# Channel mixers: inner tiles 6 to 19 all by seven block products, one weight pair's low half by an adding transfer, the residual parked in DRAM

## The chip, the cores and the metric

The kernel runs on one core of a Trainium2 chip. The metric is device microseconds (us) of one execution. TensorE (PE) multiplies, with its weight loads shown apart as PEld; VectorE (DVE) and ScalarE (ACT) do elementwise work; GpSimd (POOL) and SyncE (SP) here mostly start transfers (DMAs), which all run on the core's 16 DMA engines. Each engine works through its own instruction queue strictly in order. The order in a queue is set when the program is built and does not change at run time.

## What is computed

Two layers on a sequence of 512 positions and 1024 channels. Each has a mixer (layer 0: a recurrent one, layer 1: chunked attention) and then a channel mixer, which is where the change is:

```
def conv_glu(h, w_in, conv_w, conv_b, w_out):
    gate, val = jnp.split(h @ w_in, 2, axis=-1)
    gp = jnp.pad(gate, ((0, 0), (CONV_W - 1, 0), (0, 0)))
    conv = conv_b + sum(conv_w[j] * gp[:, j:j + seq] for j in range(CONV_W))
    return (jax.nn.gelu(conv, approximate=False) * val) @ w_out
...
        x = x + jnp.concatenate([mix, mo], axis=-1) @ w_out[layer]
        x = x + conv_glu(rms_norm(x, ln2[layer]), ffn_in[layer], ffn_conv[layer],
                         ffn_conv_b[layer], ffn_out[layer])
```

The inner width is 2816, that is 22 inner tiles of 128 columns, each with a gate block and a value block of `h @ w_in`. Everything is float32.

## The kernel before

Channels lie on the 128 partitions, positions along the free dimension. A float32 product is made of three matmuls in a faster format (`fp32r`): every operand is split into a high half (a cast, ACT) and a low half (operand minus high half, DVE), and high x high, high x low and low x high are added up in PSUM. `split_w` does this for weights, into buffers `whi` and `wlo` of 1024 columns; three of each rotate. `load_w` loads a weight block into `wraw` (two rotate) and splits it.

`ffn(l, ...)` is the channel mixer of layer `l`. Its loop over the inner tiles `j` has two bodies:

- `plain(j)`: gate and value each as one dense product over all 1024 channels, 24 matmuls of 512 columns each, 48 together. Two weight blocks are loaded and split.
- `seven(j)`: gate and value as a 2x2 block product by a Strassen-like scheme with seven block products (`prod`), 12 matmuls of 256 columns each, 84 together. The four weight blocks G1, V1, G2, V2 (512 columns each) are loaded into a buffer `raw` with room for seven blocks (two such buffers rotate); DVE makes the sums S1 and S3 (line 431, one instruction over two blocks), S2 (line 432) and S4 (line 435); S4 is written over V1. Then the operands are split: three pairs of blocks (1024 columns each) and S4 (512 columns). The four results pass through PSUM banks f1 to f4, and DVE adds them up (lines 443 to 454). The products run in the order G1, S2, S3, S1, V2, G2, S4; below they are P1 to P7.

Tiles 0 to 5 are plain (on the not yet normalised input), as meanwhile `normed` prepares the block sums of the input; of tiles 6 to 19, eleven go by `seven` and tiles 9, 13 and 17 are plain; 20 and 21 are plain. Then the 22 hidden tiles are split (`halves`), and eight output tiles follow, each with three weight loads and 66 matmuls; its result is added to the residual `xT` (line 496), 16 KB on each partition, which lies in SBUF all the time.

A buffer that rotates is loaded again only when its last reader is done. For `raw` the last reader is the split of S4, and V1, the first block to be loaded, lies in the same place. So the load for a tile waits on SP for the DVE half of the S4 split two `seven` tiles earlier. The loads run on SP's queue, in order. A scheduler that works while the program is built, with its own estimates of durations, decides how the instructions of neighbouring tiles are interleaved in each engine's queue.

An adding transfer is already in use elsewhere (`split_w` with `src`, in the projections of layer 0): ACT writes the operand with its sign turned, rounded to `fp32r` like the high half, into `wlo`, and a transfer started by POOL adds the operand, read again from DRAM, to it. This takes the subtraction from DVE.

Of the kernel before, what the change touches and what calls it, by code (L numbers as in the profile page):

```python
# [10 lines left out]
F32 = mybir.dt.float32  # L11
F32R = mybir.dt.float32r
AF = mybir.ActivationFunctionType
ALU = mybir.AluOpType
# [4 lines left out]
P = 128  # L19
S = 512  # L20
KD = 8
# [90 lines left out]
def trunk_kernel(ctx, tc, A, out):  # L112
    nc = tc.nc
    PE, V, SC, GP = nc.tensor, nc.vector, nc.scalar, nc.gpsimd
# [239 lines left out]

    PLAIN_RAW, BY_SEVEN = 6, (6, 7, 8, 10, 11, 12, 14, 15, 16, 18, 19)
    T1, T3, T2, T4 = range(4)

    def normed(k4, l, hp, xT, Nh, Nl, Mh, Ml):  # L360

        x2 = [tmp() for _ in range(2)]
        for u in range(2):
            k = k4 + 4 * u
            V.scalar_tensor_tensor(x2[u][:], xT[:, k], Vc(f"ln2_{l}", k), rho[:], op0=ALU.mult, op1=ALU.mult)
            split_to(Nh[:, k], Nl[:, k], x2[u][:])
        q = lambda i: x2[i // 2][:, i % 2 * 256:i % 2 * 256 + 256]
        su = hp.tile([P, 7, S], F32, name="raw", tag="raw", bufs=2)[:].rearrange("p a s -> p (a s)")[:, 0:1024]
        s_ = [su[:, i * 256:(i + 1) * 256] for i in range(4)]
        V.tensor_tensor(s_[T1], q(1), q(0), op=ALU.subtract)  # L370
        V.tensor_tensor(s_[T3], q(1), q(3), op=ALU.subtract)
        V.tensor_tensor(s_[T2], q(3), s_[T1], op=ALU.subtract)
        V.tensor_tensor(s_[T4], q(2), s_[T2], op=ALU.subtract)
        split_to(*(t[:, 2 * k4:2 * k4 + 2].rearrange("p a s -> p (a s)") for t in (Mh, Ml)), su)

    def ffn(l, hp, U, M, N, new_u, xT, after, last=None):


        (Uh, Ul), (Mh, Ml), (Nh, Nl) = U, M, N
        sp = hp.tile([P, 7, S], F32, name="sp", tag="sp")  # L380
        hid32 = {j: sp[:, j] for j in range(6)}

        def conv(g, j):
            c = tmp()
            SC.activation(c[:], g, AF.Identity, scale=Vc(f"cw2_{l}", j), bias=Vc(f"cb_{l}", j))
            conv_rest(c, g, j)
            return c

        def conv_rest(c, g, j):
            V.scalar_tensor_tensor(c[:, 1:S], g[:, 0:S - 1], Vc(f"cw1_{l}", j), c[:, 1:S], op0=ALU.mult, op1=ALU.add)  # L390
            V.scalar_tensor_tensor(c[:, 2:S], g[:, 0:S - 2], Vc(f"cw0_{l}", j), c[:, 2:S], op0=ALU.mult, op1=ALU.add)  # L391
            SC.activation(c[:], c[:], AF.Gelu)  # L392

        def plain(j, act, normed_):
            wg = load_w(A["ffn_in"][l, j, 0])
            wv = load_w(A["ffn_in"][l, j, 1])
            pg = ps_f()
            run(dense(pg[:], [(wg, K8)], act))
            pv = ps_f()
            run(dense(pv[:], [(wv, K8)], act))  # L400
            if normed_:
                c = conv(pg[:], j)
                V.tensor_tensor(hid32[j], pv[:], c[:], op=ALU.mult)
                return
            g = tmp()
            V.tensor_tensor(g[:], pg[:], rho[:], op=ALU.mult)
            c = conv(g[:], j)
            v = tmp()
            V.tensor_tensor(v[:], pv[:], rho[:], op=ALU.mult)
            V.tensor_tensor(hid32[j], v[:], c[:], op=ALU.mult)  # L410

        XN = lambda k0, h: [tuple(t[:, k0 + k, h * 256:h * 256 + 256] for t in (Nh, Nl)) for k in range(4)]
        XT = lambda i: [tuple(t[:, 2 * k + i // 2, i % 2 * 256:i % 2 * 256 + 256] for t in (Mh, Ml)) for k in range(4)]

        def prod(ps, w, x):
            (wh, wl), o = w
            for k in range(4):
                for n in range(2):
                    PE.matmul(ps, wh[:, o + k * P:o + k * P + P], x[k][n], start=k == n == 0, stop=False)  # L419
            for k in range(4):  # L420
                PE.matmul(ps, wl[:, o + k * P:o + k * P + P], x[k][0], start=False, stop=k == 3)  # L421

        def seven(j):

            raw = hp.tile([P, 7, S], F32, name="raw", tag="raw", bufs=2)
            g_, v_ = A["ffn_in"][l, j, 0], A["ffn_in"][l, j, 1]
            G1, S2, V2, G2, S3, S1, V1 = range(7)
            S4 = V1
            for o, src in ((V1, v_[:, 0:S]), (G1, g_[:, 0:S]), (V2, v_[:, S:2 * S]), (G2, g_[:, S:2 * S])):
                nc.sync.dma_start(raw[:, o], src)  # L430
            V.tensor_tensor(raw[:, S3:S1 + 1], raw[:, G1:V2 + 1:2], raw[:, V1:V1 + 1].to_broadcast([P, 2, S]), op=ALU.add)
            V.tensor_tensor(raw[:, S2], raw[:, S1], raw[:, G1], op=ALU.add)
            two = lambda o: split_w(raw[:, o:o + 2].rearrange("p a s -> p (a s)"), 1024)
            w_g1s2, w_s3s1, w_v2g2 = two(G1), two(S3), two(V2)
            V.tensor_tensor(raw[:, S4], raw[:, S2], raw[:, G2], op=ALU.add)
            w_s4 = split_w(raw[:, S4], S)
            h1, h2 = slice(0, 256), slice(256, 512)
            f1, f2, f3, f4 = (ps_f() for _ in range(4))
            g, c, v = tmp(), tmp(), tmp()
            prod(f1[:, h1], (w_g1s2, 0), XN(0, 0))  # L440
            SC.copy(g[:, h1], f1[:, h1])
            prod(f2[:, h1], (w_g1s2, S), XT(T2))
            V.tensor_tensor(g[:, h2], g[:, h1], f2[:, h1], op=ALU.subtract)
            prod(f1[:, h2], (w_s3s1, 0), XT(T3))
            V.tensor_tensor(c[:, h1], f1[:, h2], g[:, h2], op=ALU.subtract)

            prod(f3[:, h2], (w_s3s1, S), XT(T1))
            prod(f3[:, h1], (w_v2g2, 0), XT(T4))
            V.tensor_tensor(g[:, h2], g[:, h2], f3[:, h2], op=ALU.subtract)
            V.tensor_tensor(v[:].rearrange("p (a s) -> p a s", a=2), c[:, h1].unsqueeze(1).to_broadcast([P, 2, 256]),  # L450
                            f3[:].rearrange("p (a s) -> p a s", a=2), op=ALU.add)
            prod(f4[:, h1], (w_v2g2, S), XN(4, 0))
            prod(f4[:, h2], (w_s4, 0), XN(4, 1))
            V.tensor_tensor(g[:], g[:], f4[:], op=ALU.add)
            SC.activation(c[:], g[:], AF.Identity, scale=Vc(f"cw2_{l}", j), bias=Vc(f"cb_{l}", j))
            conv_rest(c, g[:], j)
            V.tensor_tensor(hid32[j], v[:], c[:], op=ALU.mult)

        hid = {}

        def halves(j, h, lo):
            hid[j] = h, lo
            split_to(h, lo, hid32[j])

        for j in range(PLAIN_RAW):
            plain(j, pair_of(Uh, Ul), False)
            if j < 4:
                normed(j, l, hp, xT, Nh, Nl, Mh, Ml)
        u32 = [new_u(i, F32) for i in range(2)]
        for j in range(6, NFF):  # L470
            hid32[j] = u32[(j - 6) // 8][:, (j - 6) % 8]
        for j in range(PLAIN_RAW, NFF):
            if j in BY_SEVEN:
                seven(j)
            else:
                plain(j, pair_of(Nh, Nl), True)
            if j == NFF - 2:
                hl = [hp.tile([P, 7, S], F32R, name="hl", tag="raw", bufs=2) for _ in range(2)]
                for k in range(8, 15):
                    halves(k, hl[0][:, k - 8], hl[1][:, k - 8])  # L480
        for k in range(8):
            halves(k, Mh[:, k], Ml[:, k])
        uh = new_u(0, F32R)
        sl = hp.tile([P, 7, S], F32R, name="sl", tag="sp")
        for k in range(15, NFF):
            halves(k, uh[:, k - 15], sl[:, k - 15])
        for m in range(KD):
            us = []
            for lo, n in ((8, 7), (0, 8), (15, 7)):
                us.append((load_w(A["ffn_out"][l, m][:, lo * P:(lo + n) * P], n * P), list(range(lo, lo + n))))  # L490
            if m == KD - 1 and last is not None:
                last(us, lambda k: hid[k])
                break
            ps = ps_d()
            run(dense(ps[:], us, lambda k: hid[k]))
            V.tensor_tensor(xT[:, m], xT[:, m], ps[:], op=ALU.add)  # L496
            after(m)
# [627 lines left out]
    with tc.issue_after(norm_at[0].ins):  # L1125
# [5 lines left out]
        for m in range(KD):  # L1131
            src = memT[m // 4][:, m % 4]
# [49 lines left out]
    actx.close()  # L1182

    mid = ctx.enter_context(tc.tile_pool(name="mid", bufs=1))
    xT = mid.tile([P, KD, S], F32, name="xT")
    r2h = mid.tile([P, KD, S], F32R, name="r2h")
    r2l = mid.tile([P, KD, S], F32R, name="r2l")
    for m in range(0, KD, 2):
# [336 lines left out]
```

## Time and profile before

| | |
|---|---|
| median of three runs | 1336.96 us (1335.99 to 1339.73) |
| the profiled execution | 1339.11 us; its span on the core 1337.0 us; mean granted PE clock 0.994 |
| PE busy / PEld busy | 98% / 82% of the span |
| DVE / ACT / POOL busy | 69% / 51% / 2% |
| channel mixers, tiles 6 to 19 | layer 0 from 457.7 to 601.5 us, layer 1 from 1036.9 us |

The profile is one execution. Engine rows give busy time; a row of the timeline gives an instruction's start, its duration, and in square brackets how long its engine sat idle before it and what ended the idle time. DVE and ACT instructions overlap a little, so that what an instruction costs its queue is the distance from its start to the next start, some 0.08 us less than its duration. A transfer's row gives when it was issued; the time to landing counts from there.

### The profile page before, as it was taken

How to read it: one execution, taken by the hardware profiler on the slowest of the kernel's cores; microseconds unless marked ns; L12 is line 12 of the kernel's file. 1: busy time of each engine (PE TensorE's matmuls, PEld its weight loads, DVE VectorE, ACT ScalarE, POOL GpSimd, SP SyncE). 2: the span in 40 equal slices, each digit the busy share in tenths (PEclk: the TensorE clock that was granted, in tenths of full speed). 3: DMA queues.
4: the chain of work that ended last, by engine and by line, in shares of the span. 5: the costliest groups of instructions: out<-in, count | busy, mean ns of one | idle time of the engine just before them, and what ended most of it. 6: DMA issues, size and time to landing. Idle time of an engine off the chain costs nothing. (4 is left out here: it accounts for less than half of the span.)

```text
span 1337.0 us, 24400 instructions
## 1 busy us (share of the span) xinstructions
PE 1309.7 (98%) x9838; PEld 1101.1 (82%) x9838; DVE 924.7 (69%) x1820; ACT 683.3 (51%) x1164; POOL 20.2 (2%) x45
## 2 busy tenths in 40 slices
PE   8999999999999999999999999999999999999996
PEld 7787777777688899998888877786888999988886
DVE  6967767766669898887343675757689888893224
ACT  6566666665445445464232576657454544562221
POOL 0000000000000000000000000000000000000000
PEclk9999999999999999999999999999999999999998
DMA  5374444351232424213333322232324323223332
GB/s 197 107 185 98 101 91 104 86 114 56 95 104 86 143 95 127 73 65 94 97 104 105 119 87 95 87 119 64 106 84 142 113 78 105 85 76 101 102 87 77
DMA packets 65009, 135.41 MB, mean 101 GB/s; under 512 B 19584, under 2 KB 25088, under 8 KB 64896
## 3 DMA queue, kind: packets, MB, share of 16 engines
q1 hardware_dynamic: 62448, 124.94, 30.3%
q0 software_dynamic: 2448, 8.91, 3.6%
q8 instruction: 77, 1.26, 0.4%
q14 instruction: 36, 0.29, 0.1%
HBM read 127.53 MB, written 6.29 MB: 100 GB/s over the span
## 5 line engine op out<-in xcount | busy, mean ns | idle before, releaser
L175 DVE TENSOR_TENSOR wlo<-wraw,whi 128x1024 fp32r<-128x1024 f32 (+1 forms) x139 | 165.5, 1191 | 142.3 <-PE psd L207 131.1
L169 ACT CAST whi<-wraw 128x1024 fp32r<-128x1024 f32 (+1 forms) x156 | 160.0, 1027 | 171.3 <-DMA wraw<-in_ffn_out_dram 52.6
L203 PE MATMUL psd<-r1h,whi 128*128 128x512 f32 (+1 forms) x399 | 159.2, 400 | 0.8 <-DVE xT L349 0.8
L204 PE MATMUL psd<-r1l,whi 128*128 128x512 f32 x336 | 132.2, 394 | 0.0
L169 ACT CAST whi<-raw 128x1024 fp32r<-128x1024 f32 x88 | 82.8, 942 | 79.6 <-PE psf L419 44.5
L207 PE MATMUL psd<-r1h,wlo 128*128 128x512 f32 (+1 forms) x399 | 107.0, 395 | 0.0
L175 DVE TENSOR_TENSOR wlo<-raw,whi 128x1024 fp32r<-128x1024 f32 x88 | 95.7, 1088 | 15.2 <-ACT whi L169 15.2
L203 PEld LDWEIGHTS psd<-r1h,whi 128*128 128x128 f32 x399 | 75.1, 188 | 18.7 <-issue 2.7
L207 PEld LDWEIGHTS psd<-r1h,wlo 128*128 128x128 f32 x399 | 72.1, 188 | 14.6 <-issue 0.3
L203 PE MATMUL psd<-r2h,whi 128*128 128x512 f32 (+1 forms) x200 | 77.4, 391 | 0.1
L419 PE MATMUL psf<-r2h,whi 128*128 128x256 f32 x308 | 77.2, 283 | 0.0
L419 PE MATMUL psf<-r2l,whi 128*128 128x256 f32 x308 | 77.2, 283 | 0.0
L204 PE MATMUL psd<-r2l,whi 128*128 128x512 f32 (+1 forms) x200 | 76.3, 384 | 0.8 <-DVE r2l L221 0.8
L204 PEld LDWEIGHTS psd<-r1l,whi 128*128 128x128 f32 x336 | 63.3, 188 | 11.2 <-issue 0.2
L237 ACT ACTIVATE tmp<-xT 128x512 f32<-128x512 f32 x27 | 17.0, 631 | 101.7 <-DVE xT L496 86.5
L419 PEld LDWEIGHTS psf<-r2l,whi 128*128 128x128 f32 x308 | 59.1, 192 | 0.2
L419 PEld LDWEIGHTS psf<-r2h,whi 128*128 128x128 f32 x308 | 59.1, 192 | 0.2
L207 PE MATMUL psd<-r2h,wlo 128*128 128x512 f32 (+1 forms) x200 | 50.9, 386 | 0.0
L421 PE MATMUL psf<-r2h,wlo 128*128 128x256 f32 x308 | 49.5, 283 | 0.0
L392 ACT ACTIVATE tmp<-tmp 128x512 f32<-128x512 f32 x44 | 27.7, 629 | 32.8 <-DVE tmp L391 32.4
L203 PEld LDWEIGHTS psd<-r2h,whi 128*128 128x128 f32 x200 | 37.6, 188 | 8.4 <-issue 1.2
L203 PE MATMUL psd<-hl,whi 128*128 128x512 f32 (+1 forms) x119 | 44.4, 377 | 0.0
(460 smaller groups left out, 3291.2 us busy)
## 6 DMA issues: line engine op xcount, KB each, us to landing
wraw<-in_ffn_in_dram SPq DMA_DIRECT2D x44, 512.0 KB, 3.7
raw<-in_ffn_in_dram SPq DMA_DIRECT2D x88, 256.0 KB, 4.1
wraw<-in_ffn_out_dram SPq DMA_DIRECT2D x32, 448.0 KB, 3.4
wraw<-in_wA_dram SPq DMA_DIRECT2D x20, 512.0 KB, 4.3
wraw<-in_w_out_dram SPq DMA_DIRECT2D x16, 512.0 KB, 3.8
wraw<-in_ffn_out_dram SPq DMA_DIRECT2D x16, 512.0 KB, 3.6
wlo<-in_wA_dram POOLq DMA_DIRECT2D x15, 512.0 KB, 6.9
wraw<-in_wB_dram SPq DMA_DIRECT2D x8, 512.0 KB, 3.7
```

Source lines behind the costliest of these rows:

```text
L169: SC.copy(hi[:, :n], raw)
L175: V.tensor_tensor(lo[:, :n], raw, hi[:, :n], op=ALU.subtract)
L203: PE.matmul(ps, wh[:, j * P:(j + 1) * P], ah, start=start and n == 0, stop=False)
L204: dense_at[0] = PE.matmul(ps, wh[:, j * P:(j + 1) * P], al, start=False, stop=False)
L207: dense_at[0] = PE.matmul(ps, wl[:, j * P:(j + 1) * P], act(k)[0], start=False, stop=stop and n == len(ks) - 1)
L237: SC.activation(sq[:], src, AF.Square)
L392: SC.activation(c[:], c[:], AF.Gelu)
L419: PE.matmul(ps, wh[:, o + k * P:o + k * P + P], x[k][n], start=k == n == 0, stop=False)
L421: PE.matmul(ps, wl[:, o + k * P:o + k * P + P], x[k][0], start=False, stop=k == 3)
```

## The change

1. All of tiles 6 to 19 go by `seven`: 14 instead of 11 in each layer, and three plain ones fewer.
2. In `seven` the pair G2, V2 is no longer split by `split_w`. ACT casts the pair (`hi`), ACT writes the second half from it a second time with scale -1 (`lo`), and a transfer started by POOL adds the pair, read from DRAM, to `lo` (512 KB, two rows of 2 KB on each partition). `whi` and `wlo` then serve three splits a tile (S2 with G1, S3 with S1, S4) instead of four. The blocks in `raw` change places; the products keep their order.
3. The place for `hi` and `lo` is the residual's: a buffer `side` of 16 KB a partition, with two slots for alternating tiles. Before tile 6 the residual is written to DRAM (`spill`, four transfers of 512 KB on SP's queue), and after tile 20 is issued it is read back (`fetch`, four transfers on SP's queue, which wait for the last reader of `side`).

```
-    PLAIN_RAW, BY_SEVEN = 6, (6, 7, 8, 10, 11, 12, 14, 15, 16, 18, 19)
+    PLAIN_RAW, BY_SEVEN = 6, tuple(range(6, 20))
...
+        xsp = dp.tile([P, KD, S], F32, name="xsp", tag="xsp")
+        side = []
+        def spill():
+            for m in range(0, KD, 2):
+                nc.sync.dma_start(xsp[:, m:m + 2], xT[:, m:m + 2])
+            side.append(xT.place(F32R))
+        def fetch():
+            xT.place(F32)
+            for m in range(0, KD, 2):
+                nc.sync.dma_start(xT[:, m:m + 2], xsp[:, m:m + 2])
+        def split_side(raw, src, u):
+            hi, lo = (side[0][:, o:o + 2] for o in (4 * u, 4 * u + 2))
+            SC.copy(hi, raw)
+            SC.activation(lo, raw, AF.Copy, scale=-1.0)
+            GP.dma_start(lo, src, accum_op=ALU.add)
+            return tuple(t.rearrange("p a s -> p (a s)") for t in (hi, lo))
...
-            G1, S2, V2, G2, S3, S1, V1 = range(7)
+            S2, G1, G2, V2, S3, S1, V1 = range(7)
...
+            w_g2v2 = split_side(raw[:, G2:V2 + 1], A["ffn_in"][l, j][:, :, S:2 * S].rearrange("a p s -> p a s"), j % 2)
...
-            w_g1s2, w_s3s1, w_v2g2 = two(G1), two(S3), two(V2)
+            w_s2g1, w_s3s1 = two(S2), two(S3)
...
+        spill()
         u32 = [new_u(i, F32) for i in range(2)]
...
             if j == NFF - 2:
+                fetch()
```

How the queues move. The names end in a buffer number; `raw_6173`, `raw_6299` and `raw_6425` are tiles 10, 11 and 12 before. DVE before, in layer 0, between the S4 split of tile 10 and that of tile 11 (lines 443 to 454 add up the products of the tile that PE is at):

```order
L175 TENSOR_TENSOR wlo_6194<-raw_6173,whi_6193 128x512
L445 TENSOR_TENSOR tmp_6202<-psf_6197,tmp_6201 128x256
L175 TENSOR_TENSOR wlo_6307<-raw_6299,whi_6306 128x1024
L449 TENSOR_TENSOR tmp_6201<-tmp_6201,psf_6199 128x256
L450 TENSOR_TENSOR tmp_6203<-tmp_6202,psf_6199 128x512
L431 TENSOR_TENSOR raw_6425<-raw_6425 128x1024
L175 TENSOR_TENSOR wlo_6311<-raw_6299,whi_6310 128x1024
L454 TENSOR_TENSOR tmp_6201<-tmp_6201,psf_6200 128x512
L175 TENSOR_TENSOR wlo_6315<-raw_6299,whi_6314 128x1024
L390 SCALAR_TENSOR_TENSOR tmp_6202<-tmp_6201,vec_67,tmp_6202 128x511
L175 TENSOR_TENSOR wlo_6320<-raw_6299,whi_6319 128x512
```

The first row releases a `raw` buffer to tile 12, whose sums (line 431) stand five rows on, ahead of the next release (last row). DVE now, in the same place of the program; lines 455, 456 and 459 are the old 431, 432 and 435; 467 to 478 the old 443 to 454; 481 the old 457. `raw_6108` is tile 9, `raw_6233` tile 10, and PE is at tile 8, whose S4 split stands four rows ahead of this piece:

```order
L175 TENSOR_TENSOR wlo_6119<-raw_6108,whi_6118 128x1024
L481 TENSOR_TENSOR uh_5731<-tmp_5887,tmp_5886 128x512
L469 TENSOR_TENSOR tmp_6011<-psf_6006,tmp_6010 128x256
L455 TENSOR_TENSOR raw_6233<-raw_6233 128x1024
L175 TENSOR_TENSOR wlo_6123<-raw_6108,whi_6122 128x1024
L473 TENSOR_TENSOR tmp_6010<-tmp_6010,psf_6008 128x256
L474 TENSOR_TENSOR tmp_6012<-tmp_6011,psf_6008 128x512
L456 TENSOR_TENSOR raw_6233<-raw_6233 128x512
L459 TENSOR_TENSOR raw_6233<-raw_6233 128x512
L478 TENSOR_TENSOR tmp_6010<-tmp_6010,psf_6009 128x512
L175 TENSOR_TENSOR wlo_6128<-raw_6108,whi_6127 128x512
```

One split of 1024 columns is gone, and all three sums of a tile two ahead now stand between one S4 split and the next. The same rows return for each tile up to 17.

ACT now, in the same place: the two new instructions for tile 10 (lines 441 and 442, written into `xT`, the name of the shared place) stand behind the second cast for tile 9 and ahead of its S4 cast:

```order
L169 CAST whi_6118<-raw_6108 128x1024
L392 ACTIVATE tmp_5886<-tmp_5886 128x512
L169 CAST whi_6122<-raw_6108 128x1024
L441 CAST xT_5730<-raw_6233 128x1024
L442 ACTIVATE xT_5730<-raw_6233 128x1024
L169 CAST whi_6127<-raw_6108 128x512
L479 ACTIVATE tmp_6011<-tmp_6010,vec_67 128x512
L465 COPY tmp_6135<-psf_6131 128x256
```

Before, three casts of 1024 columns for one tile stood there instead of two for one and one for the next but one. POOL gets 14 adding transfers in each layer (line 443), one a tile, with nothing else in its queue.

SP now, around the spill in layer 0: the transfers of line 430 write pairs of residual tiles, each behind the last addition to its pair, among the weight loads of the output projection and of tiles 0 and 1:

```order
L430 DMA xsp_5233<-xT_4946 128x1024
L180 DMA wraw_5168<-in_w_out_dram 128x1024
L430 DMA xsp_5233<-xT_4946 128x1024
L180 DMA wraw_5234<-in_ffn_in_dram 128x1024
L180 DMA wraw_5240<-in_ffn_in_dram 128x1024
L430 DMA xsp_5233<-xT_4946 128x1024
L180 DMA wraw_5321<-in_ffn_in_dram 128x1024
L180 DMA wraw_5327<-in_ffn_in_dram 128x1024
L430 DMA xsp_5233<-xT_4946 128x1024
L180 DMA wraw_5408<-in_ffn_in_dram 128x1024
```

Before, the loads stood there alone. The four transfers of the fetch stand behind the weight loads of tile 21 and ahead of those of the first output tile. The loads of `raw` keep their place: one tile's four behind the four of the tile before.

More of the change, by code (lines that the diff above doesn't have):

```diff
@@ L439, in seven @@
             g, c, v = tmp(), tmp(), tmp()
-            prod(f1[:, h1], (w_g1s2, 0), XN(0, 0))
+            prod(f1[:, h1], (w_s2g1, S), XN(0, 0))
             SC.copy(g[:, h1], f1[:, h1])
-            prod(f2[:, h1], (w_g1s2, S), XT(T2))
+            prod(f2[:, h1], (w_s2g1, 0), XT(T2))
             V.tensor_tensor(g[:, h2], g[:, h1], f2[:, h1], op=ALU.subtract)
@@ L447, in seven @@
             prod(f3[:, h2], (w_s3s1, S), XT(T1))
-            prod(f3[:, h1], (w_v2g2, 0), XT(T4))
+            prod(f3[:, h1], (w_g2v2, S), XT(T4))
             V.tensor_tensor(g[:, h2], g[:, h2], f3[:, h2], op=ALU.subtract)
@@ L451, in seven @@
                             f3[:].rearrange("p (a s) -> p a s", a=2), op=ALU.add)
-            prod(f4[:, h1], (w_v2g2, S), XN(4, 0))
+            prod(f4[:, h1], (w_g2v2, 0), XN(4, 0))
             prod(f4[:, h2], (w_s4, 0), XN(4, 1))
@@ L1184, in trunk_kernel, with place, __getitem__ @@
     mid = ctx.enter_context(tc.tile_pool(name="mid", bufs=1))
-    xT = mid.tile([P, KD, S], F32, name="xT")
+    class Residual:
+        def place(self, dt):
+            t_ = mid.tile([P, KD, S], dt, name="xT", tag="xT")
+            if dt is F32:
+                self.t = t_
+            return t_
+        def __getitem__(self, i):
+            return self.t[i]
+    xT = Residual()
+    xT.place(F32)
     r2h = mid.tile([P, KD, S], F32R, name="r2h")
```

## The prediction

> **What bounds the kernel now.** I read the page's busy shares first, then who PE waits for in the stretch of layer 0's channel mixer, then that stretch cut by tiles.
>
> ```profile
> span 1337.0 us, 24400 instructions
> ...
> PE 1309.7 (98%) x9838; PEld 1101.1 (82%) x9838; DVE 924.7 (69%) x1820; ACT 683.3 (51%) x1164; POOL 20.2 (2%) x45
> ```
> ```profile
> PE psd L1288 <- DVE tmp L1250: 1.0, 1, 1.0
> ```
> ```profile
> core 0: us, PE busy (x) PEld busy (x) DVE busy (x) ACT busy (x) POOL busy (x), PEclk, DMA share, GB/s
> 498.90:529.20 30.30, 30.30 (x253) 30.26 (x252) 26.34 (x38) 14.26 (x20) 0.00 (x0) 1.00 0.33 101
> 529.20:540.20 11.00, 11.00 (x51) 9.14 (x50) 9.87 (x13) 5.71 (x7) 0.00 (x0) 1.00 0.33 107
> ```
>
> PE is busy 98% of the span. The one row of waits, from 380 to 760 us, is after the mixer: in tiles 6 to 19 PE waits for nobody. The windows are three `seven` tiles and the plain tile behind them; PE is full in both, DVE at 87% and 90%. So a tile costs what PE needs for it. That is read from the starts of tiles 16, 17 (plain), 18 and 19:
>
> ```profile
> 560.40 0.28 PE L419 MATMUL psf<-r2h,whi 128*128 128x256 f32 x1
> ...
> 570.49 0.40 PE L203 MATMUL psf<-r2h,whi 128*128 128x512 f32 x1
> ...
> 581.39 0.28 PE L419 MATMUL psf<-r2h,whi 128*128 128x256 f32 x1
> ...
> 591.47 0.28 PE L419 MATMUL psf<-r2h,whi 128*128 128x256 f32 x1
> ```
>
> A `seven` tile takes 10.09 us (1.44 a product), a plain one 10.90.
>
> **Part 1, the matmuls.** Three plain tiles a layer become `seven`: 3 x 0.81 = 2.43 us a layer, **4.9 us off both layers**, if PE goes on waiting for nobody. The rest of the sum asks whether it does.
>
> **Part 2, DVE, and a ring through the loads.** DVE's queue in the middle of a chain of `seven` tiles:
>
> ```profile
> 502.60 0.68 DVE L175 TENSOR_TENSOR wlo<-raw,whi 128x512 fp32r<-128x512 f32 x1
> ...
> 508.18 1.23 DVE L431 TENSOR_TENSOR raw<-raw 128x1024 f32<-128x1024 f32 x1 [0.36 <-DMA raw<-in_ffn_in_dram]
> 509.33 1.22 DVE L175 TENSOR_TENSOR wlo<-raw,whi 128x1024 fp32r<-128x1024 f32 x1
> 510.46 0.68 DVE L454 TENSOR_TENSOR tmp<-tmp,psf 128x512 f32<-128x512 f32 x1
> 511.06 1.22 DVE L175 TENSOR_TENSOR wlo<-raw,whi 128x1024 fp32r<-128x1024 f32 x1
> 512.20 0.74 DVE L390 SCALAR_TENSOR_TENSOR tmp<-tmp,vec 128x511 f32<-128x511 f32 x1
> 512.86 0.69 DVE L175 TENSOR_TENSOR wlo<-raw,whi 128x512 fp32r<-128x512 f32 x1
> ...
> 514.12 0.41 DVE L443 TENSOR_TENSOR tmp<-tmp,psf 128x256 f32<-128x256 f32 x1
> 514.45 0.68 DVE L432 TENSOR_TENSOR raw<-raw 128x512 f32<-128x512 f32 x1
> 515.06 0.68 DVE L457 TENSOR_TENSOR uh<-tmp 128x512 f32<-128x512 f32 x1
> ```
> ```profile
> 503.31 1.76 SPq L430 DMA_DIRECT2D raw<-in_ffn_in_dram  x4
> ```
>
> From start to start an instruction costs 1.14 us at 1024 columns (the sums 1.15), 0.66 at 511, 0.60 at 512, 0.33 at 256. A tile now has two splits of 1024 and one of 512, sums of 1024, 512 and 512, three instructions of 256, three more of 512 (474, 478, 481) and two of 511: 2.28 + 0.60 + 1.15 + 1.20 + 0.99 + 1.80 + 1.32 = 9.34 us, where it was 10.48 with a third split. By work alone DVE now fits under PE's 10.09, with 0.75 to spare.
>
> But the rows also show a ring. The S4 split of tile 10 ends at 503.28, SP issues the loads of tile 12 at 503.31, and the sums of tile 12 wait for them until 508.18. Behind them stands the S4 split of tile 11, which ends at 513.55 and releases the next loads. One turn took 10.27 us, more than PE's 10.09. Before, that does no harm: the plain tile behind three turns gives PE 10.90 us of work and asks DVE for no sums. The change takes those pauses away: 12 turns follow each other (the S4 splits of tiles 6 to 17, releasing the loads of 8 to 19).
>
> A turn now is the load time L, from the end of one S4 split to the start of line 455, and DVE's work from there to the end of the next S4 split, by its new order: sums 1.15, split 1.14, lines 473 and 474 0.33 + 0.60, lines 456, 459 and 478 3 x 0.60, the S4 split 0.69: **5.71 us**. What DVE does during the load (lines 390, 391, 467, a split, 481, 469: 3.72) is hidden by it. L is read at the five places where DVE waited for it; four more pairs beside the one above:
>
> ```profile
> 461.39 0.68 DVE L175 TENSOR_TENSOR wlo<-raw,whi 128x512 fp32r<-128x512 f32 x1
> ...
> 467.47 1.23 DVE L431 TENSOR_TENSOR raw<-raw 128x1024 f32<-128x1024 f32 x1 [0.86 <-DMA raw<-in_ffn_in_dram]
> ...
> 543.74 0.69 DVE L175 TENSOR_TENSOR wlo<-raw,whi 128x512 fp32r<-128x512 f32 x1
> ...
> 549.28 1.22 DVE L431 TENSOR_TENSOR raw<-raw 128x1024 f32<-128x1024 f32 x1 [0.32 <-DMA raw<-in_ffn_in_dram]
> ```
> ```profile
> 1081.75 0.68 DVE L175 TENSOR_TENSOR wlo<-raw,whi 128x512 fp32r<-128x512 f32 x1
> ...
> 1087.69 1.23 DVE L431 TENSOR_TENSOR raw<-raw 128x1024 f32<-128x1024 f32 x1 [0.72 <-DMA raw<-in_ffn_in_dram]
> ...
> 1122.89 0.68 DVE L175 TENSOR_TENSOR wlo<-raw,whi 128x512 fp32r<-128x512 f32 x1
> ...
> 1128.93 1.23 DVE L431 TENSOR_TENSOR raw<-raw 128x1024 f32<-128x1024 f32 x1 [0.81 <-DMA raw<-in_ffn_in_dram]
> ```
>
> L is 5.40, 4.90, 4.85, 5.26 and 5.36, mean 5.15. So a turn lasts 5.15 + 5.71 = 10.86 us even with nothing else moving, 0.77 more than PE's tile.
>
> The lag is first taken from slack. Call x how long after PE's start on a tile its S4 split ends. Tile 6's split stands behind line 409, which waits for the end of plain tile 5: x = 0.60 + 0.69 = 1.3. It grows by L + 5.71 - 10.09 a turn. PE is stopped when the next tile's second pair (S3, S1), split just behind the sums, comes late: it is there at x + L + 1.15 + 1.22 and wanted by P3 of the next tile, at 10.09 + 2 x 1.44 = 12.97. So PE waits once x is over 10.60 - L, and from then on loses the whole excess at every turn.
>
> **Part 3, the adding transfers.** 14 a layer, in the same stretch as those loads. POOL starts one when ACT is through lines 441 and 442 (two passes of 1.05), which wait for the tile's last block and for the slot, free at P6 two tiles earlier. With x small that is 8.64 + 2.1 = 10.7 us after a tile's start, so 0.65 us into the next; later it moves with the load.
>
> ```profile
> L169 ACT CAST whi<-raw 128x1024 fp32r<-128x1024 f32 x14 | 14.7, 1051 | 17.7 <-PE psf L419 12.4 <-PE psf L204 4.7 <-PE psf L421 0.3
> ```
> ```profile
> wraw<-in_ffn_in_dram SPq DMA_DIRECT2D x44, 512.0 KB, 3.7
> ...
> wraw<-in_wA_dram SPq DMA_DIRECT2D x20, 512.0 KB, 4.3
> ...
> wlo<-in_wA_dram POOLq DMA_DIRECT2D x15, 512.0 KB, 6.9
> ```
> ```profile
> wraw<-in_wA_dram SPq DMA_DIRECT2D x1, 512.0 KB, 5.1
> ```
> ```profile
> q0 software_dynamic: 2448, 8.91, 3.6%
> ```
> ```profile
> L173 POOL DMA_DIRECT2D wlo<-in_wA_dram x15: 862/862/1005, 89.4 to 268.6; - x15
> DMA to landing us min/median/max: 5.7/6.9/8.0
> ```
>
> POOL is busy 0.86 us, the transfer lands after 5.7 to 8.0, so its pair is there by 8.7 us into that tile, 7 us ahead of P5 of the tile that wants it: not late. Its price is on the loads beside it. In layer 0's projections, where 17 such transfers run, a plain 512 KB load lands after 4.3 in the middle and 5.1 in the window from 127 to 142 us, where the adding transfer was issued first; 3.7 where none runs. So they add c = 0.6 to 1.4 us. The bounds are 0 (more traffic makes no load faster) and 3.6% x 1337 / 17 = 2.83 us, the full time of all 16 engines for one adding transfer. In a settled turn it is issued 0.4 + 2.1 us behind the load of its own tile, at L + 2.5 of a turn of L + 5.71, so it is 3.2 us old, of the 6.9 that it takes, when the next tile's load is issued: half of it meets that load. Where the chain starts, nearly all of it does. I take **c = 0.8**, between the median and the largest of the near rows.
>
> With L = 5.95, x grows by 1.57: 1.3 at tile 6, 2.07 at 7 (no adding transfer meets that load), 3.64, then 5.21 at 9, over 4.65 by 0.56. Tiles 10 to 17 lose 1.57 each: 0.56 + 8 x 1.57 = 13.1 us a layer, **26.2 in all**.
>
> By the Trainium skill (DMA: Bandwidth & Descriptors, Issuing engines are not separate DMA queues) transfers from SP and from GpSimd interleave on the same 16 engines, and another issuing engine saves only issue time. The 5.1 us against 3.7 agrees. It speaks against c = 0, and if a load met a whole adding transfer, c would be near the upper bound above.
>
> **Part 4, spill and fetch: 0.** The nearest rows:
>
> ```profile
> xT<-in_xT_dram SPq DMA_DIRECT2D x4, 512.0 KB, 5.7
> out_dram<-wraw SPq DMA_DIRECT2D x4, 512.0 KB, 3.2
> ```
>
> The last spill waits on SP for the last addition of the output projection; behind it stand the loads of plain tile 2, which PE wants 21.8 us later, against 3.2 + 3.7 and two splits of 1 us. The fetch waits for P6 of tile 19; the output tiles' loads behind it are wanted 23 us on, against some 4 x 3.2 for the fetch and 3.7 for a load. Were that cover gone, each would cost some 3 us a layer. ACT has one more pass of 1.05 a tile, and was half idle.
>
> **The sum**: -4.9 + 26.2 = +21.3 us on the profiled execution's 1339.1; on the median, 2.1 below it, 1337.0 + 21.3 = **1358.3**.
>
> **Rivals.**
> - *The full gain*: the ring doesn't bind, since loads issued in a settled rhythm come sooner, or DVE reaches them later. It decides from L = 10.09 - 5.71 = 4.38 down, and gives 1332.1. For it: DVE's work fits with 0.75 us to spare. Against: the smallest of five L is 4.85.
> - *The ring alone, c = 0*: x passes 5.45 at tile 12 by 0.47, five turns of 0.77 follow: 4.3 a layer, 8.6 - 4.9 = +3.7, 1340.7. With L = 4.85 only 0.7 a layer is lost (1333.5), with 5.40 7.3 (1346.7). For it: 1 MB of loads and 512 KB added fill only part of a turn.
> - *Heavier contention*: with c = 1.4, PE stops from tile 9 on, 19.7 a layer, 1371.5; at the bound of 2.83, 35.5 a layer, 1403.
>
> **How the numbers follow.** A measurement of this kernel can tell about 0.3%, 4 us, from no change. The full gain 0.13; the ring with next to no contention, within 4 us, 0.17; the ring with c from 0.3 to 1.4 0.61 (from 1347 to 1371.5 its own range); heavier 0.09. Faster 0.13, same 0.17, slower 0.70. The range from 1332 to 1372 takes in the case of the other sign and leaves out the heavy one.
>
> **What would show it.** Right: line 455 waits for the loads of `raw` at nearly every tile, a microsecond or more; PE waits at line 419 or 421 for DVE's `wlo` once a tile from about tile 9 or 10, in both layers; settled tiles take about 11.7 us; the loads of `raw` take longer to land. Wrong: windows of PE without gaps, 10.09 a tile, and no wait at line 455. The second rival shows as tiles of 10.9 from tile 12 on.

## The result, and the profile after

| | before | after |
|---|---|---|
| median of the runs beside each other | 1338.24 (1335.99 to 1339.73) | 1376.16 (1371.82 to 1377.18) |
| ratio, 95% interval | | 1.0274 (1.0256 to 1.0291) |
| profiled execution, its span | 1339.1, 1337.0 | 1377.18, 1375.4 |

The change makes the kernel 37.9 us slower. The forecast was 21.3 us slower, at 1358.3, with a range up to 1372: the right sign and the right ring, but 16.6 us too small, so that the time lies 4 us outside the range.

The page of the changed kernel (busy shares, the sums' group, the landing times of the loads and of the adding transfers):

```profile
span 1375.4 us, 25072 instructions
...
PE 1318.6 (96%) x10054; PEld 1117.4 (81%) x10054; DVE 935.8 (68%) x1852; ACT 718.2 (52%) x1210; POOL 54.0 (4%) x73
...
L455 DVE TENSOR_TENSOR raw<-raw 128x1024 f32<-128x1024 f32 x28 | 34.3, 1225 | 48.1 <-DMA raw<-in_ffn_in_dram 44.0
...
raw<-in_ffn_in_dram SPq DMA_DIRECT2D x112, 256.0 KB, 4.8
...
xT<-in_ffn_in_dram POOLq DMA_DIRECT2D x28, 512.0 KB, 5.9
```

DVE now stands idle 44.0 us at the sums of line 455, waiting for loads, and those land after 4.8 us in the middle. Before, it was 4.1:

```profile
raw<-in_ffn_in_dram SPq DMA_DIRECT2D x88, 256.0 KB, 4.1
```

What PE waits for in each layer's mixer (in order: what, total, times, longest), and DVE in layer 0's:

```profile
PE psf L419 <- ACT tmp L465: 13.9, 9, 2.6
...
PE psf L419 <- ACT tmp L465: 15.5, 10, 3.4
...
DVE raw L455 <- DMA raw<-in_ffn_in_dram: 19.3, 10, 3.2
```

Before, PE waited for nobody there. The windows of tiles 6 to 19 of layer 0, of all that lies between the two stages, and of tiles 6 to 19 of layer 1:

```profile
core 0: us, PE busy (x) PEld busy (x) DVE busy (x) ACT busy (x) POOL busy (x), PEclk, DMA share, GB/s
456.55:618.40 161.85, 147.91 (x1177) 146.07 (x1176) 132.10 (x194) 89.29 (x120) 14.31 (x12) 0.97 0.50 126
618.40:1054.20 435.80, 430.92 (x2146) 348.43 (x2145) 274.38 (x539) 223.59 (x413) 4.79 (x14) 1.00 0.35 110
1054.20:1218.86 164.66, 149.16 (x1178) 147.09 (x1177) 132.62 (x195) 89.25 (x120) 14.34 (x12) 0.96 0.49 123
```

The first two of these windows in the kernel before:

```profile
457.80:601.54 143.74, 143.74 (x1070) 138.00 (x1069) 124.77 (x175) 73.83 (x100) 0.00 (x0) 1.00 0.28 91
601.54:1037.00 435.46, 430.80 (x2146) 348.46 (x2145) 276.53 (x541) 221.74 (x412) 1.96 (x12) 1.00 0.32 100
```

14 tiles of 10.09 us would be 141.3. The two stages lose 20.6 and 23.4 us against that; 13.1 each was forecast. Between them nothing moved (435.80, before 435.46); the first begins 1.25 us earlier than before.

One turn of the ring, with its end on ACT and PE (three cuts of the timeline):

```profile
504.50 0.68 DVE L175 TENSOR_TENSOR wlo<-raw,whi 128x512 fp32r<-128x512 f32 x1
...
512.12 1.22 DVE L455 TENSOR_TENSOR raw<-raw 128x1024 f32<-128x1024 f32 x1 [2.65 <-DMA raw<-in_ffn_in_dram]
...
516.65 0.68 DVE L478 TENSOR_TENSOR tmp<-tmp,psf 128x512 f32<-128x512 f32 x1
517.25 0.69 DVE L175 TENSOR_TENSOR wlo<-raw,whi 128x512 fp32r<-128x512 f32 x1
```
```profile
517.43 0.81 ACT L479 ACTIVATE tmp<-tmp,vec 128x512 f32<-128x512 f32 x1 [2.19 <-DVE tmp L478]
518.15 0.35 ACT L465 COPY tmp<-psf 128x256 f32<-128x256 f32 x1
```
```profile
515.77 0.64 PE L421 MATMUL psf<-r1h,wlo 128*128 128x256 f32 x4
518.55 0.39 PE L419 MATMUL psf<-r1h,whi 128*128 128x256 f32 x1 [2.14 <-ACT tmp L465]
```

S4 split, loads, sums, S4 split: as forecast. But PE is not stopped by a split. P3 writes the other half of the bank from which ACT's line 465 copies P1's result, and waits for that copy; the copy stands in ACT's queue behind line 479, which waits for DVE's line 478, the last step but one of the turn. So the lateness of the load reaches PE by way of two other engines.

### The profile page after: what moved, and what is told of

Same layout as the page of the kernel before. It is cut to its first block, busy times and chain, and to the rows that moved or that the text cites. A ratio compares the mean times of both kernels' runs of the same rounds, so it can differ in the third digit from the quotient of the medians.

```text
span 1375.4 us, 25072 instructions
## 1 busy us (share of the span) xinstructions
PE 1318.6 (96%) x10054; PEld 1117.4 (81%) x10054; DVE 935.8 (68%) x1852; ACT 718.2 (52%) x1210; POOL 54.0 (4%) x73
## 3 DMA queue, kind: packets, MB, share of 16 engines
q0 software_dynamic: 10064, 23.60, 10.4%
## 5 line engine op out<-in xcount | busy, mean ns | idle before, releaser
L175 DVE TENSOR_TENSOR wlo<-wraw,whi 128x1024 fp32r<-128x1024 f32 (+1 forms) x127 | 150.7, 1187 | 143.0 <-PE psd L207 112.1
L169 ACT CAST whi<-wraw 128x1024 fp32r<-128x1024 f32 (+1 forms) x144 | 147.4, 1025 | 163.0 <-PE psd L204 44.6
L169 ACT CAST whi<-raw 128x1024 fp32r<-128x1024 f32 (+1 forms) x84 | 75.7, 901 | 36.7 <-PE psf L419 32.4
L175 DVE TENSOR_TENSOR wlo<-raw,whi 128x1024 fp32r<-128x1024 f32 (+1 forms) x84 | 87.5, 1041 | 0.9 <-ACT whi L169 0.7
L419 PE MATMUL psf<-r2l,whi 128*128 128x256 f32 x280 | 73.4, 292 | 0.0
L419 PEld LDWEIGHTS psf<-r2h,whi 128*128 128x128 f32 x280 | 56.3, 201 | 17.6 <-ACT tmp L465 17.5
L455 DVE TENSOR_TENSOR raw<-raw 128x1024 f32<-128x1024 f32 x28 | 34.3, 1225 | 48.1 <-DMA raw<-in_ffn_in_dram 44.0
L441 ACT CAST xT<-raw 128x1024 fp32r<-128x1024 f32 x28 | 29.4, 1049 | 60.1 <-DMA raw<-in_ffn_in_dram 31.1
L419 PE MATMUL psf<-r1h,whi 128*128 128x256 f32 x168 | 46.1, 303 | 13.9 <-ACT tmp L465 13.9
L443 POOL DMA_DIRECT2D xT<-in_ffn_in_dram x28 | 33.4, 1194 | 544.3 <-ACT xT L442 532.7
```

What stands on the lines that cost most here:

```text
L169: SC.copy(hi[:, :n], raw)
L175: V.tensor_tensor(lo[:, :n], raw, hi[:, :n], op=ALU.subtract)
L441: SC.copy(hi, raw)
L443: GP.dma_start(lo, src, accum_op=ALU.add)
```

## The experiments

Each edit below is made to the changed kernel. The mean L and turn are over the 12 turns of each layer (first layer, second layer), from the end of one S4 split to the sums that wait for its loads, and to the end of the next S4 split. L is left out where the sums do not stand waiting for the load between two S4 splits, and both where plain tiles lie between the turns:

| kernel | median us | its own before | ratio (95%) | L | turn |
|---|---|---|---|---|---|
| changed kernel | 1376.16 | 1338.24 | 1.0274 (1.0256 to 1.0291) | 6.11, 6.31 | 11.86, 12.06 |
| half the adding transfer | 1360.00 | 1339.01 | 1.0155 (1.0134 to 1.0176) | 5.40, 5.71 | 11.15, 11.46 |
| no adding transfer | 1349.81 | 1338.94 | 1.0081 (1.0067 to 1.0095) | 4.82, 5.23 | 10.58, 10.99 |
| copy behind P3 | 1365.35 | 1338.94 | 1.0192 (1.0178 to 1.0206) | 6.00, 5.99 | 11.68, 11.69 |
| filler matmuls | 1377.88 | 1338.94 | 1.0292 (1.0278 to 1.0306) | 6.06, 6.15 | 11.89, 11.98 |
| tied on DVE | 1366.77 | 1338.94 | 1.0212 (1.0198 to 1.0226) | | 11.43, 11.55 |
| tied on ACT | 1352.93 | 1339.01 | 1.0094 (1.0064 to 1.0124) | 5.55, 5.99 | 10.70, 11.14 |
| tied on both | 1335.13 | 1339.46 | 0.9967 (0.9956 to 0.9979) | | 10.16, 10.15 |
| both, copy behind P3 | 1334.07 | 1339.46 | 0.9956 (0.9944 to 0.9969) | | 10.08, 10.08 |
| no side pair | 1346.20 | 1339.46 | 1.0053 (1.0039 to 1.0067) | | 10.91, 10.94 |
| tiles 9, 13, 17 plain | 1361.40 | 1339.46 | 1.0163 (1.0148 to 1.0179) | | |

### Breaking the ring on DVE

```diff
-            V.tensor_tensor(raw[:, S3:S1 + 1], raw[:, G1:V2 + 1:2], ...
+            with tc.issue_after(s4_at[0].ins) if j > PLAIN_RAW else ExitStack():
+                V.tensor_tensor(raw[:, S3:S1 + 1], raw[:, G1:V2 + 1:2], ...
...
+            s4_at[0] = split_at[0]     # DVE's S4 split of this tile
```

> One order on DVE is added: line 455's sums of a tile are issued only behind the S4 split of the tile before, so that the next loads are issued a whole turn of DVE's work (9.34 us) before their sums; the adding transfers, the spill and the fetch stay. Theory A (the ring of loads, sums and S4 split sets the time, and PE stands at P3 for ACT's copy of line 465): a load of up to 8.6 us is hidden, the waits of DVE for loads at the sums and of PE for line 465 go, a tile takes PE's 10.09 us, and the whole is 1332 to 1336. Theory B (the adding transfer's own traffic, or ACT's two more passes a tile, hold PE up): both are still there, so 1360 or more. Theory C (the granted clock, once it has fallen, is part of the cost): it falls only behind waits of PE, so it is 1.00 throughout and the time as by A.

Measured: 1366.77, only 9.4 us off the changed kernel, so not theory A's 1332 to 1336 but in the range of theory B. DVE waits for no load any more, yet the ring goes on. Waits of ACT and DVE in layer 0, and ACT's queue:

```profile
ACT xT L443 <- DMA raw<-in_ffn_in_dram: 34.1, 12, 4.2
...
DVE wlo L177 <- ACT whi L171: 23.0, 12, 3.5
```
```profile
523.62 1.05 ACT L443 CAST xT<-raw 128x1024 fp32r<-128x1024 f32 x1 [2.56 <-DMA raw<-in_ffn_in_dram]
524.57 1.05 ACT L444 ACTIVATE xT<-raw 128x1024 fp32r<-128x1024 f32 x1
525.53 0.60 ACT L171 CAST whi<-raw 128x512 fp32r<-128x512 f32 x1
```

(Line numbers here are 2 to 4 higher than in the changed kernel.) The side pair's passes wait for the same loads, and behind them in ACT's queue stands the cast for the S4 split of the tile before: load, two passes of 0.95 us, cast, S4 split, next load. The ring had a second way through, on ACT, that I had not written down; with the first closed it set the time. This run alone can't tell that from a cost of ACT's passes and of the transfers themselves; the run with both ties, further on, can. Its turn is long because POOL now starts each transfer just ahead of the loads (0.93 us before the S4 split's end at 526.85):

```profile
525.92 1.20 POOL L445 DMA_DIRECT2D xT<-in_ffn_in_dram  x1 [10.08 <-ACT xT L444]
```

and the loads land after 6.3 us in the middle:

```profile
raw<-in_ffn_in_dram SPq DMA_DIRECT2D x112, 256.0 KB, 6.3
```

### Leaving the adding transfer out, and halving it

```diff
-            GP.dma_start(lo, src, accum_op=ALU.add)
+            GP.dma_start(lo[:, 0:1], src[:, 0:1], accum_op=ALU.add)    # the halved one
```

> The adding transfer is left out (the low half of the two blocks is then only minus the raw weights); all else stays. Theory A: the ring alone, c = 0: L about 5.15, turns of 10.86 us instead of the 11.96 measured, so 1.1 x 24 = 26 us less than the changed kernel: about 1350, with waits of PE at line 465 that begin some tiles later. The prediction's own working with its later deadline gives 1340.7. Theory B (ACT's two more passes at lines 441 and 442, not the transfer, delay line 465 and the turn): within 5 us of the changed kernel, 1371 or more. Theory C (the adding transfer is the whole cost, there is no ring without it): 1332.

> The adding transfer moves only one of the two blocks, 256 KB of 512 (the other block's low half is then only minus the raw weights); all else as in the changed kernel. Theory A with contention by bytes: half of the 1.1 to 1.3 us a turn that leaving the transfer out saved, so turns of about 11.3 and 1361 to 1365. If the cost is one of the transfer's start and not of its bytes: 1372 or more. If half the bytes pass before the next loads begin and meet none of them: 1350 to 1354.

Measured: 1349.81, where theory A has about 1350, and 1360.00, 1 us below the 1361 to 1365 that it has for the half. L means 5.03, 5.56 and 6.21 us with 0, 256 and 512 KB added beside it: the adding transfer lengthens the loads about in proportion to its bytes, by 1.18 us for the whole one. A ring without any adding transfer still loses: layer 0's stage without it,

```profile
458.20:604.60 146.40, 143.83 (x1177) 141.59 (x1176) 131.77 (x193) 88.54 (x119) 0.00 (x0) 1.00 0.29 92
```

is 5.1 us over 141.3. Of the 42.8 us that the changed kernel lies above the full gain (1376.16 - 1338.24 + 4.9), 26.3 (1376.16 - 1349.81) come with the adding transfers, the rest from the ring alone.

How much a load is lengthened hangs on how old the transfer is when the load is issued. POOL's start of two transfers in the changed kernel, and the S4 split and the sums on DVE that follow each:

```profile
491.01 1.19 POOL L443 DMA_DIRECT2D xT<-in_ffn_in_dram  x1 [11.22 <-ACT xT L442]
...
527.91 1.20 POOL L443 DMA_DIRECT2D xT<-in_ffn_in_dram  x1 [11.69 <-ACT xT L442]
```
```profile
493.20 0.68 DVE L175 TENSOR_TENSOR wlo<-raw,whi 128x512 fp32r<-128x512 f32 x1
...
499.37 1.23 DVE L455 TENSOR_TENSOR raw<-raw 128x1024 f32<-128x1024 f32 x1 [1.20 <-issue]
```
```profile
528.18 0.68 DVE L175 TENSOR_TENSOR wlo<-raw,whi 128x512 fp32r<-128x512 f32 x1
...
536.44 1.23 DVE L455 TENSOR_TENSOR raw<-raw 128x1024 f32<-128x1024 f32 x1 [3.22 <-DMA raw<-in_ffn_in_dram]
```

2.87 us old, L is 5.49; 0.95 us old, L is 7.58. Over all 24 turns: behind the three transfers 0.93 to 1.05 us old L is 7.07 to 8.55, in the mean 7.73, that is 2.7 us over the 5.03; behind the eleven that are 2.77 to 2.93 us old it is 5.08 to 6.51, in the mean 5.52, 0.5 over it. Single loads scatter: without any adding transfer two loads of layer 1 took 6.78 and 6.06, and why stays open. The 8.55 is 3.5 us over the mean, more than the 2.83 that the prediction took for the upper bound. That bound was read from transfers of another form (144 packets each; the new ones have 272). By the same row of the changed kernel's page (10.4% of 1375.4 us, less the 3.6% of 1337.0 before, for 28 transfers) the new ones take an estimated 3.4 us of all 16 engines each.

### The copy behind the third product

```diff
-            SC.copy(g[:, h1], f1[:, h1])
             prod(f2[:, h1], (w_s2g1, 0), XT(T2))
-            V.tensor_tensor(g[:, h2], g[:, h1], f2[:, h1], op=ALU.subtract)
             prod(f1[:, h2], (w_s3s1, 0), XT(T3))
+            SC.copy(g[:, h1], f1[:, h1])
+            V.tensor_tensor(g[:, h2], g[:, h1], f2[:, h1], op=ALU.subtract)
```

> ACT's copy of the first product (line 465) and the subtraction behind it are put behind the third product, so PE need not wait for that copy before P3; the loads, the sums, the splits and the adding transfers are as in the changed kernel. Theory A: the ring's turn stays at about 11.96 us, and only the slack before PE is stopped grows, from x = 6.7 - L to about 10.6 - L: some 4 us a layer, 8 to 9 in all, so 1367 to 1369; PE's waits move from line 465 to the splits of DVE. Theory B (the copy of line 465, queued behind the gelu chain on ACT, is itself what sets the tiles' length): the loss goes and the time is 1340 or less. Theory C (the order of the two has no weight): 1376.

Measured: 1365.35, 10.8 off (8 to 9 expected). The turns stay near 11.7: the ring isn't touched, PE is only stopped later in it. It now stops about once in two turns, mostly just as DVE's line 469 ends behind the sums (PE, then DVE; the profile names ACT's cast, which ends at nearly the same moment, but puts one such stop, of 3.49 us in layer 1, down to line 469). Three of the 13 stops are at DVE's `wlo`, as the prediction had it:

```profile
499.28 0.36 PE L419 MATMUL psf<-r1h,whi 128*128 128x256 f32 x1 [2.73 <-ACT xT L441]
```
```profile
497.57 1.23 DVE L455 TENSOR_TENSOR raw<-raw 128x1024 f32<-128x1024 f32 x1 [3.15 <-DMA raw<-in_ffn_in_dram]
498.71 0.42 DVE L469 TENSOR_TENSOR tmp<-psf,tmp 128x256 f32<-128x256 f32 x1
```

### Filling PE's waits

In the changed kernel the granted clock fell behind some waits of PE (windows just behind the waits of 2.14, 1.40, 3.38 and 2.70 us):

```profile
518.55:524.00 5.45, 5.45 (x33) 5.45 (x34) 4.58 (x7) 2.59 (x3) 0.00 (x0) 0.69 0.87 259
566.20:572.00 5.80, 5.78 (x48) 5.78 (x49) 4.01 (x8) 2.59 (x3) 0.00 (x0) 1.00 0.96 261
...
1141.40:1147.00 5.60, 5.55 (x26) 5.55 (x27) 3.69 (x7) 2.45 (x4) 0.00 (x0) 0.50 0.97 265
...
1178.60:1184.00 5.40, 5.39 (x45) 5.39 (x46) 4.08 (x7) 2.59 (x3) 0.00 (x0) 1.00 0.86 259
```

Does this cost time of its own? The filler:

```diff
             prod(f2[:, h1], (w_s2g1, 0), XT(T2))
+            dm = ps_s()
+            for _ in range(12):
+                PE.matmul(dm[:, 0:256], w_s2g1[0][:, 0:P], XT(T2)[0][0], start=True, stop=True)
```

> Ahead of the third product of each tile 6 to 19 PE is given 12 more matmuls of 256 columns into a free bank (12 x 0.12 = 1.44 us, the result is not used), 1.44 x 28 = 40.3 us of work, which the waits of PE can take up (29.4 us of waits are at line 465, some more at other lines). Theory A: the ring sets the settled turns (11.96 us against 11.53 of PE's work with the filler), so the extra work goes into the waits there and adds only where PE wasn't yet waiting, some 2 x 4 to 8 us before the lag has built up, less what the shorter time to that point takes off the wait: 1374 to 1386. Theory C (the granted clock of 0.66 to 0.95 behind waits of over 1.8 us costs up to 12 us of its own): the clock stays at 1.00 with the filler, and the time falls to 1364 to 1370. Theory B (PE's own work sets the tiles): 1376 + 40 = 1416.

Measured: 1377.88 against 1376.16, with 40.3 us more work on PE and the clock held up. PE's waits in layer 0, and its stage:

```profile
PE psf L419 <- ACT tmp L465: 1.5, 2, 1.1
```
```profile
457.60:621.80 164.20, 162.69 (x1348) 161.98 (x1347) 135.71 (x196) 88.98 (x121) 14.31 (x12) 1.00 0.50 123
```

The work went into the waits, the turns stayed at 11.89 and 11.98. So in the changed kernel the fallen clock cost no time that these runs can tell: PE's slower matmuls ran in time that the ring would have taken anyway. That holds only while the ring sets the tiles; the run with tiles 9, 13 and 17 plain, further on, shows the other case.

### Ties on both engines, and on ACT alone

```diff
-            w_g2v2 = split_side(raw[:, G2:V2 + 1], ...
+            with tc.issue_after(s4_at[1].ins) if j > PLAIN_RAW else ExitStack():
+                w_g2v2 = split_side(raw[:, G2:V2 + 1], ...
...
-            s4_at[0] = split_at[0]
+            s4_at[:] = split_at[0], cast_at[0]     # and ACT's cast for it
```

> As in the run with the order tied on DVE, and ACT's two side passes (which wait for the same loads) are now also issued only behind ACT's cast for the S4 split of the tile before. In that run DVE no longer waited for loads, but the ring had moved to ACT: its side pass waited 2.5 to 4.2 us a tile for the load with the cast for S4 behind it, and turns took 11.43 and 11.55 us. Theory A (the ring, wherever it passes, is the cost): with no wait for loads left between two S4 splits, tiles take PE's 10.09 us or DVE's 9.34 and the time is 1332 to 1338. Theory B (the adding transfers and the two more passes cost something of their own): still 1355 or more.

> Both ties, and ACT's copy of the first product put behind the third product. Theory A: if the ring is gone there is no wait for that copy left to save, and the time is that of the run with both ties, 1332 to 1338, within 3 us. If PE still stood at that copy with both ties, it is faster than that run by what the copy cost.

> Only ACT's side passes are tied behind ACT's cast for the S4 split of the tile before; DVE's order is free, so line 455's sums stand ahead of the S4 split of the tile before again. Theory A: the ring closes through DVE as in the changed kernel (L + 5.71 a turn), and the side passes, now later, start the adding transfer nearer to the next loads, which lengthens L: turns of 11.9 to 13, 1374 or more. Theory B (ACT's side passes, waiting for loads, are the place where the time goes): with them out of the way, 1340 or less.

Measured: with both ties 1335.13, 0.9967 (0.9956 to 0.9979) of before, with all adding transfers and passes in place. With the copy moved as well 1334.07, the fastest of all; the two agree within 1.1 us, as expected. DVE, two turns with both ties; what it and PE wait for; the loads:

```profile
498.56 0.68 DVE L177 TENSOR_TENSOR wlo<-raw,whi 128x512 fp32r<-128x512 f32 x1
499.17 1.22 DVE L459 TENSOR_TENSOR raw<-raw 128x1024 f32<-128x1024 f32 x1
...
508.64 0.69 DVE L177 TENSOR_TENSOR wlo<-raw,whi 128x512 fp32r<-128x512 f32 x1
509.25 1.22 DVE L459 TENSOR_TENSOR raw<-raw 128x1024 f32<-128x1024 f32 x1
```
```profile
DVE tmp L483 <- PE psf L423: 9.6, 13, 1.6
...
PE psf L421 <- ACT tmp L470: 0.8, 1, 0.8
```
```profile
raw<-in_ffn_in_dram SPq DMA_DIRECT2D x112, 256.0 KB, 3.9
```

The loads issued at 499.27 are wanted at 509.25. DVE waits for PE again instead of the other way round, and a tile is 10.08 us.

With the tie on ACT alone I was wrong: 1374 or more was expected, 1352.93 came. Two sizes moved that I took as fixed. In this order one of the three sums of 512 columns (line 462 there) goes behind the S4 split, so the turn's work is 5.16 instead of 5.75 us. And POOL starts the transfer behind the loads (SP's issue of the loads, then POOL):

```profile
503.33 34.34 SPq L455 DMA_DIRECT2D raw<-in_ffn_in_dram  x16
```
```profile
505.12 1.20 POOL L445 DMA_DIRECT2D xT<-in_ffn_in_dram  x1 [9.46 <-ACT xT L444]
```

so that L is 5.55 and 5.99. It is still a ring: turns of 10.70 and 11.14.

### Parts of the change alone

```diff
-            w_g2v2 = split_side(raw[:, G2:V2 + 1], ...
-            w_s2g1, w_s3s1 = two(S2), two(S3)
+            w_s2g1, w_s3s1, w_g2v2 = two(S2), two(S3), two(G2)
...
-        spill()
...
-                fetch()
```
```diff
-    PLAIN_RAW, BY_SEVEN = 6, tuple(range(6, 20))
+    PLAIN_RAW, BY_SEVEN = 6, (6, 7, 8, 10, 11, 12, 14, 15, 16, 18, 19)
```

> The first part of the change alone: all 14 tiles by seven products, the third weight pair split on DVE as before the change, no side pair, no adding transfers, no spill and fetch. DVE's work is then 10.48 us a tile, more than PE's 10.09. Theory A: a ring with no contention, with the third split (1.14 us) inside the turn or beside the load by DVE's order: turns of 10.5 (all DVE work, no wait) to 12.0 (L = 5.15 + 5.71 + 1.14), so with 24 turns and 8.8 us of slack in all, up to -4.9 + 24 x 1.9 - 8.8 = +32: 1342 to 1371, the middle likelier. Theory B (the adding transfers are the whole cost): DVE's 10.48 a tile alone, 24 x 0.39 = 9.4, less the slack and the 4.9: 1333 to 1338.

> The side pair, the adding transfers, the spill and the fetch for the tiles by seven products, but tiles 9, 13 and 17 plain, as before the change. Theory A: the ring's lag is reset by a plain tile after three turns at most; in the changed kernel PE stopped from the third seven tile on (1.05 and 0.57 us in tiles 7 and 8 of layer 0), so a group of three costs 1 to 2 us at its end, 4 groups x 2 layers: 1337 to 1348. Theory B (each adding transfer costs something of its own, 40 us over 28): 22 of them cost 31 us, 1368.

Without the side pair: 1346.20, in the lower part of theory A's range. With three splits DVE has so much to do that in the later turns the loads are there before the sums; turns settle at 10.72, near DVE's 10.48 of work. From 537.49 to 591.07, five such turns, DVE is busy 53.12 of 53.58 us: it is the bound there, not the ring. So seven products in all tiles, without the side pair, cost 6.7 us.

Three tiles at a time, with the side pair: 1361.40, where 1337 to 1348 was expected. A miss. The last turn of a group in layer 0 (POOL, DVE, PE):

```profile
510.76 1.20 POOL L443 DMA_DIRECT2D xT<-in_ffn_in_dram  x1 [18.87 <-ACT xT L442]
```
```profile
512.05 0.68 DVE L175 TENSOR_TENSOR wlo<-raw,whi 128x512 fp32r<-128x512 f32 x1
...
521.14 1.23 DVE L455 TENSOR_TENSOR raw<-raw 128x1024 f32<-128x1024 f32 x1 [4.12 <-DMA raw<-in_ffn_in_dram]
```
```profile
527.57 0.39 PE L419 MATMUL psf<-r1h,whi 128*128 128x256 f32 x1 [3.88 <-ACT tmp L465]
```

L is 8.41 beside a transfer 2 us old, and one such load stops PE at once; no lag has to build up. The end of each group of three stopped PE for 1.99 to 3.88 us, where 1 to 2 was expected. Why this load is longer than the 6.2 to 7.2 us beside transfers of that age in the changed kernel wasn't tried; two other loads of this run, beside transfers as old, took 6.50 and 6.58.

The stops explain two thirds. Layer 0's stage is 156.25 us long where it was 143.74 before, with the same 1070 matmuls. PE is idle in 8.4 of the 12.5 us more; the other 4.1 are longer matmuls (busy 147.84, before 143.74). The granted clock was 0.69 over the 5.5 us behind the wait of 3.88 and 0.70 over the 5.1 us behind one of 2.26. The plain tile that follows leaves no wait to take this up, so here the fallen clock costs time.

## Why the prediction was right and wrong

- **Part 1** held: with the ring gone 4.3 and 5.4 us came off (1339.46 less 1335.13 and 1334.07), 4.9 forecast.
- **The ring of part 2** held: its steps, its length beside L (5.75 us measured, 5.71 forecast), DVE's waits at line 455 in nearly every turn, and the proof that the time comes back when it is broken in both queues.
- **The slack of part 2 failed.** "PE is stopped when the next tile's second pair (S3, S1), split just behind the sums, comes late ... So PE waits once x is over 10.60 - L". I took the pair of splits just behind the sums for the first thing in the turn that PE wants. In the trace P3 resumes at 518.55, 0.6 us behind the end of the turn's S4 split (517.94), because it wants ACT's copy; the pair was ready 3.5 us ahead of that end (the split behind the sums ends at 514.48). PE wants something 4 us later in the turn than I had it, so a chain has 0.5 us of slack on average and not 4.9 (the turns' excess over 10.09, 22.5 us a layer, less the 22.0 that the stages lose), and PE stops from tile 7 on (1.05 us, up to 470.71), not from 9 or 10. That is 8.8 of the 17.8 us missing from the loss of both stages. The copy run shows the same from the other side: with the copy out of P3's way 10.8 us come back while the turn stays, at 11.69 against 11.86 and 12.06.
- **Part 3's c was mis-sized**: 0.8 taken, 1.18 measured by leaving the transfer out (bounds 0 and 2.83). With the no-transfer L of 5.03 instead of 5.15, the turn is 11.96 and not 11.66. Over 12 turns of two layers, the first of which I had taken without a transfer, and with 0.04 us a turn of DVE's work, that is the other 9 us (excess over 10.09 of 22.5 us a layer, where 18.0 was forecast). The step that failed is "half of it meets that load": the transfer's age at the loads' issue swings from 1 to 4 us, since ACT's passes wait now for the load, now for P6 (12 and 14 times of 28); in the mean it is 2.4, where 3.2 was taken. With 1.18 for c and all else as in the prediction, its sum gives 1366.7, still 9.5 us short.
- **Part 4** held: 0.3 us between the stages.
- **Rivals.** The full gain's condition, L down to 4.38, came about in no kernel with the ring (the lowest mean is 4.82). The full gain came in another way, when the loads were given DVE's whole turn. The ring alone was priced at 1340.7 and measured at 1349.8, off mainly by the same slack.
- The sentence on where PE would wait named DVE's `wlo`; it was ACT's copy.

## What to carry to other kernels

In a strict-order queue, an instruction that waits for a load closes a ring if something behind it frees the buffer for the next load. Look for that in every engine that touches the buffer, because here, taken out of one queue, the ring went on through another. When pricing the slack before such a ring hurts, follow what the bounding engine wants to the last link, through shared banks and other engines' queues, not to the first product of the turn. Here one order tie on each of two engines turned 2.7% slower into 0.3% faster (0.4% with the copy moved as well). And where PE had no later wait to make up for the fallen clock, as in the run with plain tiles between, its stops cost more than their own length.

## What was not expected of the hardware

- Behind PE's waits of 1.84 to 2.55 us (five) and 3.38 the granted clock fell, to 0.67 to 0.69 and to 0.50 over the next 5.1 to 5.6 us; behind one of 2.70 and all twelve up to 1.69 it stayed at 1.00. In the run with tiles 9, 13 and 17 plain it stayed behind 1.99 and 2.64. By the Trainium skill (TensorE: Matmul & The Clock Gate, Part 1: The HAM clock gate) half rate comes after at least one idle window of some 3.4 us. Here less was enough, and not each time.
- An adding transfer of 512 KB cost a 1 MB load 2.7 us on average when the load was issued about 1 us behind it (three loads), 0.5 us at 2.8 to 2.9 us (eleven loads), and 0.7 us on average when the load was issued 1.1 to 2.3 us ahead of it, mostly 1.8 (tie on ACT: L 5.77 in the mean, over 5.03). In these runs its cost goes mostly with when it starts.
